# A two-layer decoder trunk on one core: tile starts at multiples of 512 bytes, half-tiles of the next stage ahead of the last transposes, other homes for the last groups' weights

## The chip, the core and the metric

The kernel runs on one core of one Trainium2 chip. The core has TensorE for matrix products (PE in the profile, with its weight loads as PEld), VectorE (DVE), ScalarE (ACT), GpSimd (POOL) and SyncE (SP, which here only issues DMAs). The metric is the device time of one execution in microseconds (us); lower is better. Before the change the median of three runs is 3107.32 us (3106.07 to 3114.94). Chances below speak of faster or slower by over 0.3%, which is about 9.3 us.

## The reference

The input is one sequence of 1024 positions with 1024 features, float32, and a memory of 256 tokens. Two layers follow each other; each is

```python
mix, xq = mixer(x)                                   # layer 0: gated delta rule; layer 1: S5 scan
cross = memory_attention(xq, mem, w_kv[i])           # 4 heads of 128
h = concatenate([mix, cross]) @ w_o[i]               # 1536 -> 1024
x = layer_norm(1.414 * x + h, ln1_g[i], ln1_b[i])
f = square(relu(x @ mlp_w1[i])) @ mlp_w2[i]          # 1024 -> 4096 -> 1024
x = layer_norm(1.414 * x + f, ln2_g[i], ln2_b[i])
```

The mixer of layer 0 is a gated DeltaNet (8 heads of 128, a short convolution on q, k and v, a chunked recurrence). That of layer 1 is a diagonal state-space layer (64 groups of 16 channels, a complex state of 64 each), followed by `z * sigmoid(z @ w_glu + b)`.

## The kernel before

**Arithmetic.** Large products run in the type float32r. Each operand is split into a high part `hi` (a copy rounded to float32r, by ACT) and a low part `lo` (the difference, by DVE). A product is three matmuls into the same PSUM bank (`mm3`, lines 110 to 116): hi times hi on L114, hi times lo on L115, lo times hi on L116. The moving operand is 512 columns wide, the stationary one 128 by 128. Small products (the recurrences, the S5 blocks, the transposes) are plain float32.

**Layouts.** Activations that go into a projection lie feature-major in `xT`: per half `h` of the 1024 positions a `hi` and a `lo` tile of 8 blocks of 512 columns, so four tiles. Results that are added up lie position-major in `y`, 8 blocks `tau` of 128 positions.

**Homes.** One SBUF pool holds a fixed number of buffers for each tag (`TAGS`): six `xT` of 16 KB a partition, two `raw`, four `w1`, seven `h1`, nine `h2`, seven `h3`, six `h4`, five `h5`, two `gb`, one `scr`, six `S`. A buffer is as large as the largest tile of its tag, and buffers lie one after another behind the constants. Sizes before: `s5t` (2T + 2·8·129 floats) makes an `xT` buffer 16448 bytes; the convolution's `cv` (3 + T floats) makes a `gb` buffer 4128 bytes after rounding; `H1` (4·9·16 floats) makes an `h5` buffer 2304 bytes; `scr` has 5280 bytes. As the tags follow each other, in the built program every tile of a large matmul starts at an odd multiple of 32 bytes: 224 past a multiple of 512 for `w1` and `h1`, 416 past one for `h2`, `h3` and `h4`, and 32 to 480 past one for the six `xT` buffers.

**Weights.** `load_split` (L86) reads 128 rows of a weight into a `raw` buffer (SP queue), makes one 1024-wide `hi` (ACT, L93) and `lo` (DVE, L94). `load_split2` (L98) does the same in two halves of 512 (ACT L106, DVE L107), each with a home of its own.

**Stages.** The order is: layer 0's mixer and attention (0 to about 830 us); `out_proj` of layer 0 with the first layer norm; the MLP of layer 0 (about 990 to 1771 us) with `s5_side`, which prepares tables and matrices of S5 beside the first 13 blocks; `mem_kv` and the S5 stage of layer 1 (to about 2110 us); `glu`; `out_proj` of layer 1; the MLP of layer 1 (about 2370 us to the end).

**Out projection and MLP.** `out_proj` (L798) takes the 12 row blocks of the concatenated outputs in four groups of two and a last group of four; the MLP (L186) takes the 32 blocks of 128 hidden features in 14 groups of two and a last group of four. In each group the weights are loaded, in the MLP the hidden block is projected (`proj_fm`, matmuls named `w`), and then for each `tau` two banks are summed by `acc_tm` (matmuls named `tm`) and added to `y` by DVE. In the last group each `tau` is finished by `done`: a layer norm on DVE and POOL (L160 to L170), a store where there is one, and `transpose_x` (L172), which is eight transposes on PE (`xt`, L180) and two `hi`/`lo` pairs (L182, L183) into the new `xT`. The next stage's first projection needs the new `xT`: its half 0 is there after `tau` 3, its half 1 after `tau` 7.

The order on each engine is fixed at build time by the tile framework, which follows the program's order as a priority and places an instruction where it expects its operands to be ready. At the end of layer 0's `out_proj` PE's order is: eight transposes of `tau` 6, two `w`, eight transposes, two `w`, and so on; the next group's first `w` follow behind the last transposes.

Lines that the change touches: `mlp`, `block_end`, `mlp_block`, `out_proj`, `combine`, `s5_mats`, `s5_u`, `s5_core`, `run`, and the sizes in `conv_silu` and `gdn_consts`.

Of the kernel before, what the change touches and what calls it, by code (L numbers as in the profile page):

```python
# [16 lines left out]
P = 128  # L17
# [11 lines left out]
class Trunk:  # L29
    def __init__(self, ctx, tc, a):  # L30
        self.tc = tc
        self.nc = nc = tc.nc
        self.a = a
        self.uid = 0
        self.turn = 0
        self.proj = 0
        self.cp = ctx.enter_context(tc.tile_pool(name="cp", bufs=1))
        self.sp = ctx.enter_context(tc.tile_pool(name="sp", bufs=1))
        self.ps = ctx.enter_context(tc.tile_pool(name="ps", bufs=1, space=bass.MemoryType.PSUM))
        self.dp = ctx.enter_context(tc.tile_pool(name="dp", bufs=1, space=bass.MemoryType.DRAM))  # L40
# [78 lines left out]
    def new_xT(self):  # L119
        return [tuple(self.tile("xT", [P, KT, HALF], F32R, f"xT{p}{h}") for p in "hl") for h in range(2)]  # L120

    def proj_fm(self, src, xT, evac, nm, banks=("mm",)):

        w = src if isinstance(src, tuple) else self.load_split(src, "w1", nm)
        for h in range(2):
            self.proj += 1
            ps = self.psum(banks[self.proj % len(banks)], nm)
            for k in range(KT):
                c = slice(k * P, (k + 1) * P)
                self.mm3(ps, (w[0][:, c], w[1][:, c]), (xT[h][0][:, k, :], xT[h][1][:, k, :]), k == 0, k == KT - 1)  # L130
            evac(h, ps)
# [54 lines left out]
    def mlp(self, i, xT, y, done, side=None):  # L186
        nc = self.nc
        blocks = [(2 * n, 2 * n + 1) for n in range(14)] + [(28, 29, 30, 31)]
        for fb, fs in enumerate(blocks):
            last = len(fs) == 4  # L190
            wk = [self.load_split2(self.a["w2"][i, f], ("h1", "h2", "h2", "h5")[j], "w2") for j, f in enumerate(fs)]
            hk = []
            for j, f in enumerate(fs):
                hs = [None, None]

                def evac(h, ps):
                    nc.scalar.activation(ps, ps, AF.Relu)  # L197
                    nc.scalar.activation(ps, ps, AF.Square)
                    hi = self.tile("h1" if j == 3 and h else "h3", [P, HALF], F32R, "hh")
                    lo = self.tile("h1" if j == 3 else "h4", [P, HALF], F32R, "hl")  # L200
                    nc.scalar.copy(hi, ps)  # L201
                    nc.vector.tensor_tensor(lo, ps, f32(hi), op=ALU.subtract)  # L202
                    hs[h] = (hi, lo)

                self.proj_fm(self.a["w1"][i, f], xT, evac, "w1", ("mm", "mm", "pa"))
                hk.append(hs)
            for tau in range(8):
                def add(c, ps):
                    o = y[tau][:, c * HALF:(c + 1) * HALF]
                    if fb == 0:  # L210
                        nc.vector.scalar_tensor_tensor(o, o, ALPHA, ps, op0=ALU.mult, op1=ALU.add)
                    else:
                        nc.vector.tensor_tensor(o, ps, o, op=ALU.add)  # L213
# [586 lines left out]
    def out_proj(self, i, y, done, early):  # L800
# [3 lines left out]
        for gi, ks in enumerate(order):  # L804
            last = len(ks) == 4
            wk, hk = [], []
            for j, k in enumerate(ks):
                tag = ("w1", "h5", "h2", "h2")[j] if early and last else "w1" if early and gi % 2 == 0 else \
                    ("h1", "h5")[j] if early else ("h1", "h2", "h2", "h5")[j]
                if tag == "w1":  # L810
                    hi, lo = self.load_split(self.a["w_o"][i, k], "w1", "wo")
                    wk.append([(hi[:, c * HALF:(c + 1) * HALF], lo[:, c * HALF:(c + 1) * HALF]) for c in range(2)])
                else:
                    wk.append(self.load_split2(self.a["w_o"][i, k], tag, "wo"))
            if early and not last:
                hq = self.tile("xT", [P, KT, HALF], F32R, "chl")
            for j, k in enumerate(ks):
                r = self.load_raw(self.cat[k * P:(k + 1) * P], "cat")
                hs = []
                if j == 3 and not early:  # L820
                    hq = [self.tile("w1", [P, 1024], F32R, "chl") for _ in range(2)]
                for h in range(2):
                    s = r[:, h * HALF:(h + 1) * HALF]
                    if early and not last:
                        hi, lo = hq[:, 4 * j + 2 * h, :], hq[:, 4 * j + 2 * h + 1, :]
                    elif j == 3 and not early:
                        hi, lo = (q[:, h * HALF:(h + 1) * HALF] for q in hq)
                    else:
                        hi = self.tile("h1" if j == 3 else "h3", [P, HALF], F32R, "ch")
                        lo = self.tile("h1" if j == 3 else "h4", [P, HALF], F32R, "cl")  # L830
# [171 lines left out]
    def combine(self, eng, x, y, pr, pi, op, b, nm):  # L1002

        n = pr.shape[1]
        o, w = (self.tile("h5", [P, 4, n, 16], F32, z) for z in (nm, "cw"))
# [33 lines left out]
    def s5_mats(self, m, b, co):  # L1039
# [7 lines left out]
        h1 = self.combine(V, co[:, 2], co[:, 3], re[:, :, gl], im[:, :, gl], A_, b, "H1")  # L1047
        nc.gpsimd.dma_start(self.h1d[m, :, gs], h1)
        dd = self.dd(8 * m + 4 * b)
        pz = self.psum("pa", "pz", (P, 4, 8, 16))  # L1050
        for g in range(4):
            nc.tensor.matmul(flat(pz[:16, g]), co[:, 0, 4 * b + g, :], flat(h1[:, g, 0:8, :]), start=True, stop=False)
# [14 lines left out]
    def s5_u(self, m, xT):  # L1067
        nc = self.nc
        u = self.s5t[:, 0:T]
# [4 lines left out]
        self.proj_fm(self.a["w_in5"][m], xT, evac, "wu")  # L1074
        nc.sync.dma_start(self.ud[m].rearrange("s c n -> c s n"), u.rearrange("p (s n) -> p s n", s=8))

    def s5_core(self, m):
# [4 lines left out]
        u = self.s5t[:, 2 * T + 8 * 129 * (m % 2):2 * T + 8 * 129 * (m % 2 + 1)].rearrange("p (g n) -> p g n", g=8)  # L1082
        V.memset(u[:, :, 0:1], 0.0)
        nc.sync.dma_start(u[:, :, 1:129], self.ud[m].rearrange("s (i g) n -> (s i) g n", i=16))
# [3 lines left out]
        for b in range(2):  # L1088
# [18 lines left out]
            for g in range(4):  # L1107
                nc.tensor.matmul(p1[:, g, :], G1[:, g], u[:, 4 * b + g, 0:128], start=True, stop=True)
            for g in range(4):
                nc.tensor.matmul(p2[:, g, :], G2[:, g], u[:, 4 * b + g, 0:128], start=True, stop=True)  # L1110
# [54 lines left out]
    def run(self):  # L1165
# [36 lines left out]
        xT = self.block_end(0, y)  # L1202
# [3 lines left out]
        xT = self.mlp_block(0, y, xT, self.s5_side, lambda tau: nc.sync.dma_start(self.x2[tau], y[tau]), True)  # L1206
        kv = self.mem_kv(1)
        self.s5t = self.tile("xT", [P, 2 * T + 2 * 8 * 129], F32, "s5t")
        self.s5_u(0, xT)
        for m in range(8):  # L1210
            if m < 7:
                self.s5_u(m + 1, xT)
# [7 lines left out]
        xT = self.block_end(1, y)  # L1220
        out = a["out"].rearrange("(n s) d -> s n d", s=8)
        self.mlp_block(1, y, xT, None, lambda tau: nc.sync.dma_start(out[tau], y[tau]), False)

    def block_end(self, i, y):

        xT = []

        def done(tau):
            if not xT:
                xT.extend(self.new_xT())  # L1230
# [5 lines left out]
        return xT  # L1236

    def mlp_block(self, i, y, xT, side, store, more):
        new = []

        def done(tau):
# [6 lines left out]
            if more:  # L1248
                self.transpose_x(y[tau], tau, new)

        self.mlp(i, xT, y, done, side)
# [89 lines left out]
```

## Time and profile before

| | |
|---|---|
| median of three runs | 3107.32 us |
| profiled execution | 3115.24 us |
| its span, first to last instruction | 3113.5 us |
| PE busy | 2892.1 us, 93% |
| DVE busy | 1762.9 us, 57% |
| ACT busy | 964.6 us, 31% |
| POOL busy | 488.4 us, 16% |
| mean granted TensorE clock | 0.967 of full |

Matmuls overlap in the array, so a matmul's listed duration (about 0.4 us for 512 columns) is longer than the distance from its start to the next one's. The distance, taken from starts in the timeline or from the number of matmuls in a stretch, is what adds up to time.

### The profile page before, as it was taken

The numbers are of one execution on the slowest core, as the hardware profiler recorded it, in microseconds if no ns is written. First come the engines' busy times: TensorE is split into PE (matmuls) and PEld (weight loads), VectorE is DVE, ScalarE is ACT, GpSimd is POOL, SyncE is SP. The second block draws the span as 40 slices with busy tenths as digits, with TensorE's granted clock in tenths as the row PEclk, the third lists the DMA queues.
The fourth block names the chain that finished last, engine by engine and source line by source line (L and its number), as shares of the span: only waits on it lengthen the run. The fifth ranks groups of instructions, "written<-read, shape, count | busy, mean of one in ns | idle before, by whom it ended". The sixth has DMA issues, their size and how long they took to land. (4 is left out here: it accounts for less than half of the span.)

```text
span 3113.5 us, 36492 instructions
## 1 busy us (share of the span) xinstructions
PE 2892.1 (93%) x13629; PEld 2311.9 (74%) x13629; DVE 1762.9 (57%) x3452; ACT 964.6 (31%) x2070; POOL 488.4 (16%) x729
## 2 busy tenths in 40 slices
PE   8789898898998999999999989987999999999998
PEld 6568676676777888777777767765777888888876
DVE  7635766765578677666663733443467344334436
ACT  5334444443422322232222222332222222222221
POOL 3620633625001021110100100011000000000001
PEclk9889999999999999999999999998999999999999
DMA  5322433333522133222221365554321111111111
GB/s 193 101 58 82 115 105 101 99 105 77 179 82 76 42 108 92 83 97 73 87 85 62 103 183 168 167 144 142 108 95 61 48 48 43 53 48 48 41 48 54
DMA packets 204145, 288.11 MB, mean 93 GB/s; under 512 B 85776, under 2 KB 126944, under 8 KB 203968
## 3 DMA queue, kind: packets, MB, share of 16 engines
q1 hardware_dynamic: 188864, 245.46, 25.7%
q0 software_dynamic: 12800, 36.13, 3.9%
q10 hardware_dynamic: 2304, 4.20, 0.4%
q8 instruction: 107, 1.75, 0.2%
q14 instruction: 70, 0.57, 0.1%
HBM read 213.93 MB, written 71.79 MB: 92 GB/s over the span
## 5 line engine op out<-in xcount | busy, mean ns | idle before, releaser
L213 DVE TENSOR_TENSOR y<-tm,y 128x512 f32<-128x512 f32 x448 | 308.5, 690 | 223.0 <-PE tm L116 217.4
L114 PE MATMUL w<-xTh,w1h 128*128 128x512 f32 x1024 | 409.7, 400 | 14.9 <-ACT w1h L93 14.9
L116 PE MATMUL w<-xTh,w1l 128*128 128x512 f32 x1024 | 407.4, 398 | 4.5 <-DVE w1l L94 4.4
L114 PE MATMUL tm<-w2h,hh 128*128 128x512 f32 x1024 | 406.7, 398 | 0.0
L115 PE MATMUL w<-xTl,w1h 128*128 128x512 f32 x1024 | 406.6, 397 | 0.0
L116 PE MATMUL tm<-w2h,hl 128*128 128x512 f32 x1024 | 403.6, 395 | 0.0
L115 PE MATMUL tm<-w2l,hh 128*128 128x512 f32 x1024 | 402.1, 393 | 0.0
L106 ACT CAST w2h<-w2r 128x512 fp32r<-128x512 f32 x128 | 76.3, 619 | 588.7 <-PE tm L116 506.0
L114 PEld LDWEIGHTS w<-xTh,w1h 128*128 128x128 f32 x1024 | 194.1, 190 | 60.0 <-ACT w1h L93 16.2
L116 PEld LDWEIGHTS w<-xTh,w1l 128*128 128x128 f32 x1024 | 194.5, 190 | 52.0 <-DVE w1l L94 6.3
L115 PEld LDWEIGHTS w<-xTl,w1h 128*128 128x128 f32 x1024 | 194.2, 190 | 45.1
L116 PEld LDWEIGHTS tm<-w2h,hl 128*128 128x128 f32 x1024 | 192.1, 188 | 47.4 <-DVE hl L202 0.3
L114 PEld LDWEIGHTS tm<-w2h,hh 128*128 128x128 f32 x1024 | 192.2, 188 | 45.8 <-ACT hh L201 1.3
L115 PEld LDWEIGHTS tm<-w2l,hh 128*128 128x128 f32 x1024 | 192.7, 188 | 44.7
L167 POOL TENSOR_SCALAR mv<-mv 128x1 f32<-128x1 f32 x32 | 25.0, 780 | 1246.8 <-DVE mv L166 1246.8
L202 DVE TENSOR_TENSOR hl<-w,hh 128x512 fp32r<-128x512 f32 x128 | 87.2, 687 | 188.6 <-ACT hh L201 188.6
L94 DVE TENSOR_TENSOR w1l<-w1r,w1h 128x1024 fp32r<-128x1024 f32 x64 | 78.3, 1224 | 184.7 <-ACT w1h L93 184.7
L114 PE MATMUL wi<-xTh,wih 128*128 128x512 f32 x384 | 159.3, 415 | 3.5 <-ACT zc L640 3.5
L115 PE MATMUL wi<-xTl,wih 128*128 128x512 f32 x384 | 158.7, 413 | 0.0
L116 PE MATMUL wi<-xTh,wil 128*128 128x512 f32 x384 | 156.4, 407 | 0.0
L197 ACT ACTIVATE w<-w 128x512 f32<-128x512 f32 x128 | 74.5, 582 | 188.0 <-PE w L116 188.0
L93 ACT CAST w1h<-w1r 128x1024 fp32r<-128x1024 f32 x64 | 67.2, 1050 | 198.8 <-PE w L115 157.4
(414 smaller groups left out, 5791.3 us busy)
## 6 DMA issues: line engine op xcount, KB each, us to landing
w2r<-in_w_dram SPq DMA_DIRECT2D x64, 512.0 KB, 3.5
w1r<-in_w_dram SPq DMA_DIRECT2D x64, 512.0 KB, 3.5
wir<-in_w_in_dram SPq DMA_DIRECT2D x24, 512.0 KB, 3.7
wor<-in_w_o_dram SPq DMA_DIRECT2D x24, 512.0 KB, 3.5
cat<-cat SPq DMA_DIRECT2D x24, 512.0 KB, 3.4
gb<-gcd SPq DMA_DIRECT2D x32, 256.0 KB, 4.5
ntf<-nm POOLq DMA_DIRECT2D x32, 256.0 KB, 3.0
nm<-ntf SPq DMA_DIRECT2D x32, 256.0 KB, 3.4
```

The costliest lines, as they stand in the source:

```text
L93: nc.scalar.copy(hi, r)
L94: nc.vector.tensor_tensor(lo, r, f32(hi), op=ALU.subtract)
L106: nc.scalar.copy(hi, s)
L114: nc.tensor.matmul(ps, a[0], b[0], start=start, stop=False)
L115: nc.tensor.matmul(ps, a[0], b[1], start=False, stop=False)
L116: nc.tensor.matmul(ps, a[1], b[0], start=False, stop=stop)
L167: nc.gpsimd.tensor_scalar(mv[:, 2:3], mv[:, 1:2], 1e-5, None, op0=ALU.add)
L197: nc.scalar.activation(ps, ps, AF.Relu)
L202: nc.vector.tensor_tensor(lo, ps, f32(hi), op=ALU.subtract)
L213: nc.vector.tensor_tensor(o, ps, o, op=ALU.add)
```

## The change

Four things are done.

1. **Starts.** A constant `pad` of 112 floats is added, and sizes are changed so that each buffer is a multiple of 512 bytes: `scr` 11·P floats, `cv` T + P floats, `h5` 2048 bytes, `xT` 16384 bytes. Every tile of the large matmuls then starts at a multiple of 512 bytes. For `h5`, `H1` loses its ninth power: `combine` makes powers 0 to 7 in one call and power 8 in another, with small tiles under tag `S`, and the ninth goes to `h1d` by a DMA of its own. For `xT`, `s5t` loses the zero column in front of each group's 128 inputs: `u` has 128 columns, its `memset` goes, and the two state products are added into columns 1 to 127 of `py` instead of running on a shifted input.
2. **Order at three stage ends.** `proj_fm` is split, so that half `h` can be projected alone (`proj_half`). At the last `tau` of both `out_proj` and of layer 0's MLP, `last_x` runs: half 0 of the next stage's first block (24 matmuls), then the transposes of `tau` 6, half 0 of the next stage's second block (24 matmuls), then the transposes of `tau` 7. The next stage is the MLP (`mlp_front`: two blocks of `w1`) or S5 (`u_front`: `s5_u` of blocks 0 and 1, ahead of `mem_kv`). Their halves 1 come later. The new `xT` is taken half by half.
3. **The MLP's last group.** Of the four `w2` tiles two are loaded ahead, and the other two are loaded at the fourth block, behind the loads of three `w1` tiles, where all four came ahead of them before.
4. **The out projections' last group.** The weights' tags are `h5`, `h2`, `w1`, `w1` in layer 1 (before `h1`, `h2`, `h2`, `h5`) and `w1`, `w1`, `h2`, `h2` in layer 0 (before `w1`, `h5`, `h2`, `h2`). The split inputs of half 0 lie in one `xT` buffer, those of half 1 in `h3` and `h4`.

The core of the diff:

```diff
+        self.const("pad", [P, 112])
...
+    def proj_half(self, w, xT, h, nm, banks=("mm",)):
+        self.proj += 1
+        ps = self.psum(banks[self.proj % len(banks)], nm)
+        for k in range(KT):
+            t, c = (w[k // 4], k % 4) if isinstance(w, list) else (w, k)
+            c = slice(c * P, (c + 1) * P)
+            self.mm3(ps, (t[0][:, c], t[1][:, c]), (xT[h][0][:, k, :], xT[h][1][:, k, :]), k == 0, k == KT - 1)
+        return ps
...
+    def last_x(self, y, xT, work):
+        for tau in (6, 7):
+            next(work)
+            self.transpose_x(y[tau], tau, xT)
+
+    def mlp_front(self, i, xT, front):
+        ws = [self.load_split2(self.a["w1"][i, 0], "h1", "w1"), self.load_split(self.a["w1"][i, 1], "w1", "w1")]
+        hk = [[None, None] for _ in ws]
+        for j, w in enumerate(ws):
+            self.hidden(hk[j], j)(0, self.proj_half(w, xT, 0, "w1", self.W1_BANKS))
+            if j:
+                front.extend((ws, hk))
+            yield
...
-            wk = [self.load_split2(self.a["w2"][i, f], ("h1", "h2", "h2", "h5")[j], "w2") for j, f in enumerate(fs)]
+            load_w2 = lambda j: self.load_split2(self.a["w2"][i, fs[j]], ("h1", "h2", "h2", "h5")[j], "w2")
+            wk = [load_w2(0), load_w2(1)]
+            if fb == 0:
+                ws, hk = front
+                for j, w in enumerate(ws):
+                    self.hidden(hk[j], j)(1, self.proj_half(w, xT, 1, "w1", self.W1_BANKS))
+            else:
+                hk = []
+                for j, f in enumerate(fs):
+                    if j == 3:
+                        wk += [load_w2(2), load_w2(3)]
+                    hk.append([None, None])
+                    self.proj_fm(self.a["w1"][i, f], xT, self.hidden(hk[j], j), "w1", self.W1_BANKS)
...
-        scr = self.tile("scr", [P, 3 * P + 8 + 13 * 64 + 96], F32, "scr")
+        scr = self.tile("scr", [P, 11 * P], F32, "scr")[:, :3 * P + 8 + 13 * 64 + 96]
...
-        cv = self.tile("gb", [P, 3 + T], F32, "cv")
+        cv = self.tile("gb", [P, T + P], F32, "cv")[:, :3 + T]
...
-                tag = ("w1", "h5", "h2", "h2")[j] if early and last else "w1" if early and gi % 2 == 0 else \
-                    ("h1", "h5")[j] if early else ("h1", "h2", "h2", "h5")[j]
+                if last:
+                    tag = (("w1", "w1", "h2", "h2") if early else ("h5", "h2", "w1", "w1"))[j]
+                else:
+                    tag = "w1" if early and gi % 2 == 0 else ("h1", "h5" if early else "h2")[j]
...
-            if early and not last:
+            if early or last:
                 hq = self.tile("xT", [P, KT, HALF], F32R, "chl")
...
+                    if last and h == 0:
+                        hi, lo = hq[:, 2 * j, :], hq[:, 2 * j + 1, :]
...
-        h1 = self.combine(V, co[:, 2], co[:, 3], re[:, :, gl], im[:, :, gl], A_, b, "H1")
-        nc.gpsimd.dma_start(self.h1d[m, :, gs], h1)
+        h1 = self.combine(V, co[:, 2], co[:, 3], re[:, 0:8, gl], im[:, 0:8, gl], A_, b, "H1")
+        nc.gpsimd.dma_start(self.h1d[m, :, gs, 0:8], h1)
+        h8 = self.combine(V, co[:, 2], co[:, 3], re[:, 8:9, gl], im[:, 8:9, gl], A_, b, "H8", "S")
+        nc.gpsimd.dma_start(self.h1d[m, :, gs, 8:9], h8)
...
-        V.memset(u[:, :, 0:1], 0.0)
-        nc.sync.dma_start(u[:, :, 1:129], self.ud[m].rearrange("s (i g) n -> (s i) g n", i=16))
+        nc.sync.dma_start(u, self.ud[m].rearrange("s (i g) n -> (s i) g n", i=16))
...
-                nc.tensor.matmul(py[:, g, :], M0[:, 4 * b + g, :], u[:, 4 * b + g, 1:129], start=True, stop=False)
-                nc.tensor.matmul(py[:, g, :], H1[:, g], r1[:, g, :], start=False, stop=False)
-                nc.tensor.matmul(py[:, g, :], H2[:, g], r2[:, g, :], start=False, stop=True)
+                nc.tensor.matmul(py[:, g, :], M0[:, 4 * b + g, :], u[:, 4 * b + g, :], start=True, stop=False)
+                nc.tensor.matmul(py[:, g, 1:], H1[:, g], r1[:, g, 0:P - 1], start=False, stop=False)
+                nc.tensor.matmul(py[:, g, 1:], H2[:, g], r2[:, g, 0:P - 1], start=False, stop=True)
...
+        def u_front(xT):
+            self.s5t = self.tile("xT", [P, 4 * T], F32, "s5t")
+            self.us = [self.s5_u(m, xT) for m in range(2)]
+            for u in self.us:
+                next(u)
+                yield
...
-            self.transpose_x(y[tau], tau, xT)
+            if tau == 7:
+                self.last_x(y, xT, self.mlp_front(i, xT, front))
+            elif tau < 6:
+                self.transpose_x(y[tau], tau, xT)
```

In the built program PE's order at the end of layer 0's `out_proj` becomes: 22 `tm`, 24 `w`, 8 transposes, 24 `w`, 8 transposes, one `tm`, two `w`, two `tm`, 46 `w`, 93 `tm`. At the end of layer 0's MLP it becomes 24 `wu`, 8 transposes, 24 `wu`, 8 transposes, 48 `wu`, and then the 96 `mk` of `mem_kv`, which followed the transposes directly before.

More of the change, by code (lines that the diff above doesn't have):

```diff
@@ L125, in proj_fm @@
         for h in range(2):
[L126 to L131, printed above, removed]
+            evac(h, self.proj_half(w, xT, h, nm, banks))
     def quad(self, dt, nm):
@@ L183, in transpose_x, with hidden, evac, mlp @@
             nc.vector.tensor_tensor(lo[:, 4 * q:4 * q + 4, t0:t0 + P], ps, f32(o), op=ALU.subtract)
-    def mlp(self, i, xT, y, done, side=None):
+    def hidden(self, hs, j):
+        nc = self.nc
+        def evac(h, ps):
+            nc.scalar.activation(ps, ps, AF.Relu)
+            nc.scalar.activation(ps, ps, AF.Square)
+            hi = self.tile("h1" if j == 3 and h else "h3", [P, HALF], F32R, "hh")
+            lo = self.tile("h1" if j == 3 else "h4", [P, HALF], F32R, "hl")
+            nc.scalar.copy(hi, ps)
+            nc.vector.tensor_tensor(lo, ps, f32(hi), op=ALU.subtract)
+            hs[h] = (hi, lo)
+        return evac
+    W1_BANKS = ("mm", "mm", "pa")
+    def last_x(self, y, xT, work):
[10 more added lines that the diff above has]
+            yield
+    def mlp(self, i, xT, y, done, side, front):
         nc = self.nc
@@ L819, in out_proj @@
                 hs = []
-                if j == 3 and not early:
-                    hq = [self.tile("w1", [P, 1024], F32R, "chl") for _ in range(2)]
                 for h in range(2):
                     s = r[:, h * HALF:(h + 1) * HALF]
-                    if early and not last:
+                    if last and h == 0:
+                        hi, lo = hq[:, 2 * j, :], hq[:, 2 * j + 1, :]
+                    elif early and not last:
                         hi, lo = hq[:, 4 * j + 2 * h, :], hq[:, 4 * j + 2 * h + 1, :]
-                    elif j == 3 and not early:
-                        hi, lo = (q[:, h * HALF:(h + 1) * HALF] for q in hq)
-                    else:
-                        hi = self.tile("h1" if j == 3 else "h3", [P, HALF], F32R, "ch")
-                        lo = self.tile("h1" if j == 3 else "h4", [P, HALF], F32R, "cl")
+                    else:
+                        hi = self.tile("h3", [P, HALF], F32R, "ch")
+                        lo = self.tile("h4", [P, HALF], F32R, "cl")
                     nc.scalar.copy(hi, s)
@@ L1201, in run @@
             nc.sync.dma_start(y[tau], a["x"].rearrange("(n s) d -> s n d", s=8)[tau])
[L1202 removed]
+        xT, front = self.block_end(0, y)
         self.x2 = d("x2", [8, P, T])
         self.cat = d("cat1", [1536, T])
[L1206 removed]
+        def u_front(xT):
[3 more added lines that the diff above has]
+                next(u)
+                yield
+        xT = self.mlp_block(0, y, xT, front, self.s5_side, lambda tau: nc.sync.dma_start(self.x2[tau], y[tau]), u_front)
+        for u in self.us:
+            next(u)
         kv = self.mem_kv(1)
[L1208 to L1209 removed]
         for m in range(8):
[L1211 to L1212 removed]
+            if 0 < m < 7:
+                for _ in self.s5_u(m + 1, xT):
+                    pass
             self.s5_core(m)
@@ L1247, in done @@
             store(tau)
-            if more:
+            if more and tau == 7:
+                self.last_x(y, new, more(new))
+            elif more and tau < 6:
                 self.transpose_x(y[tau], tau, new)
-        self.mlp(i, xT, y, done, side)
+        self.mlp(i, xT, y, done, side, front)
         return new
```

51 lines of the change are left out of this document (22 added, 29 removed).

## The prediction

> **What bounds the kernel now.** I read the page first (span, engines, clock, costliest groups), then a table by stretches with each engine's busy time, then PE's timeline at the places where that table shows too little work, and last single lines.
>
> ```profile
> span 3113.5 us, 36492 instructions
> ...
> PE 2892.1 (93%) x13629; PEld 2311.9 (74%) x13629; DVE 1762.9 (57%) x3452; ACT 964.6 (31%) x2070; POOL 488.4 (16%) x729
> ...
> PEclk9889999999999999999999999998999999999999
> ...
> L213 DVE TENSOR_TENSOR y<-tm,y 128x512 f32<-128x512 f32 x448 | 308.5, 690 | 223.0 <-PE tm L116 217.4
> L114 PE MATMUL w<-xTh,w1h 128*128 128x512 f32 x1024 | 409.7, 400 | 14.9 <-ACT w1h L93 14.9
> ...
> L114 PE MATMUL tm<-w2h,hh 128*128 128x512 f32 x1024 | 406.7, 398 | 0.0
> ```
>
> PE is busy 93% of the span, and DVE's commonest step, the sum into `y`, waits for PE. So PE is the bound, in two ways: how far apart its matmuls start while it is fed, and the places where it isn't. The stretches (columns: length, busy us and instructions of PE, PEld, DVE, ACT, POOL, then the granted clock, DMA share, GB/s):
>
> ```profile
> 986.00:1002.00 16.00, 8.74 (x39) 6.82 (x39) 14.42 (x20) 4.98 (x8) 4.68 (x8) 0.68 0.25 87
> 1667.00:1677.00 10.00, 4.20 (x11) 2.63 (x10) 4.94 (x7) 3.27 (x5) 0.00 (x0) 0.66 0.56 187
> 1769.00:1784.00 15.00, 8.37 (x45) 7.23 (x44) 11.84 (x19) 4.76 (x8) 2.71 (x3) 0.77 0.61 212
> 2308.00:2321.00 13.00, 7.71 (x23) 5.80 (x23) 6.66 (x11) 4.70 (x9) 0.00 (x0) 0.74 0.58 200
> 2365.00:2381.00 16.00, 9.33 (x35) 7.35 (x34) 13.50 (x18) 5.11 (x8) 2.38 (x3) 0.68 0.53 165
> 2500.00:2900.00 400.00, 400.00 (x1721) 323.27 (x1720) 165.37 (x233) 101.68 (x162) 0.00 (x0) 1.00 0.14 48
> 3003.00:3016.00 13.00, 7.14 (x19) 4.86 (x18) 5.44 (x7) 3.23 (x4) 0.00 (x0) 0.74 0.60 194
> ```
>
> The sixth row is an MLP in steady state: 1720 matmuls in 400 us, one every 232.5 ns, PE never idle, clock 1.00. The other six rows are the places the change touches: PE works about half of each, and the granted clock falls to 0.66 to 0.77 there. PE's timeline at them (start, duration, and in brackets the idle time before and who ended it):
>
> ```profile
> 986.07 1.03 PE L180 MATMUL xt<-ident,y 128*128 128x128 f32 x8
> 986.86 0.47 PE L114 MATMUL tm<-woh,ch 128*128 128x512 f32 x1
> ...
> 991.74 1.94 PE L180 MATMUL xt<-ident,y 128*128 128x128 f32 x8 [2.79 <-DVE y L170]
> 998.08 0.79 PE L116 MATMUL w<-xTh,w1l 128*128 128x512 f32 x1 [4.40 <-DVE w1l L94]
> ...
> 1673.54 0.80 PE L114 MATMUL w<-xTh,w1h 128*128 128x512 f32 x1 [5.76 <-ACT w1h L93]
> ...
> 1777.86 1.94 PE L180 MATMUL xt<-ident,y 128*128 128x128 f32 x8 [5.58 <-DVE y L170]
> ...
> 2313.73 0.80 PE L114 MATMUL tm<-woh,ch 128*128 128x512 f32 x1 [5.29 <-ACT ch L831]
> ...
> 2375.17 1.94 PE L180 MATMUL xt<-ident,y 128*128 128x128 f32 x8 [3.39 <-DVE y L170]
> ...
> 3009.49 0.80 PE L114 MATMUL w<-xTh,w1h 128*128 128x512 f32 x1 [5.83 <-ACT w1h L93]
> ```
>
> At the three stage ends (986, 1769, 2365) PE stands before transposes whose layer norm isn't done; at the three last groups (1667, 2308, 3003) it stands before weights or inputs whose split came late. To price a stretch I take from its length what its PE work would need at full speed: 0.2325 us per 512-column matmul, 0.10 per transpose (eight from 986.07 to 986.86), 0.114 per 256-column `mk` (rows below). Lost at 986: 16 less 15 matmuls and 24 transposes (3.5 + 2.4) = 10.1. At 1667: 10 less 11 matmuls = 7.4. At 1769: 15 less 8 matmuls, 16 transposes and 21 `mk` (1.9 + 1.6 + 2.4) = 9.1. At 2308: 13 less 23 = 7.7. At 2365: 16 less 19 and 16 transposes (4.4 + 1.6) = 10.0. At 3003: 13 less 19 = 8.6. Together 53 us, with the slow clock after each stall.
>
> **The change part by part: order and homes.** The split of `proj_fm` puts 24 matmuls (5.6 us) ahead of the transposes of `tau` 6 and 24 ahead of those of `tau` 7. At 986 the last `tm` ends near 988.3 and `y` of `tau` 6 is there at 991.7: the first 24 cover that. How long the next one takes is DVE's matter:
>
> ```profile
> L164 DVE BATCH_NORM_STATS2 bn<-y 128x6 f32<-128x512 f32 x64 | 42.3, 681 | 0.4
> L170 DVE SCALAR_TENSOR_TENSOR y<-y,mv,gb 128x1024 f32<-128x1024 f32 x32 | 40.9, 1278 | 2.9 <-POOL mv L168 2.9
> L183 DVE TENSOR_TENSOR xTl<-xt,xTh 128x512 fp32r<-128x512 f32 x48 | 30.8, 681 | 3.0 <-ACT xTh L182 2.6
> ```
>
> A `tau` costs DVE two sums (0.69 each), two statistics (0.68), two 1024-wide steps (1.28; L169 has L170's form) and two `lo` (0.68): 6.7 us. So `tau` 7 is ready at about 998.5, and PE, after 48 matmuls and 8 transposes from 988.3, at 1000.4: no wait. Next late is half 1, which needs the two `hi`/`lo` pairs of `tau` 7, about 2 us after the transposes. I leave 2 us at each of the three ends: 6 of 53 stay. At the last groups all loads are issued earlier or into homes that are free; I take the stalls there as gone. What hides the loads is the group before (two blocks, over 20 us of PE). If a home isn't free, 5 to 6 us come back per place.
>
> New cost on those paths: the front projections put four hidden-block `lo` (0.68 us, the form of L183) on DVE ahead of the last norms, where DVE is 14.42 of 16 us busy: 2.7 us. On SP's queue the front's `w1` loads now stand ahead of the next `w2`, and in the last group two `w2` stand behind three `w1`; they are needed only after all four projections, over 10 us later. With 1 us for the rest: 4 us. Net of this part: 53 − 6 − 4 = 43 us saved. Its ends: nothing saved at the last groups and a lost front (20) to all of 53.
>
> Elsewhere: `combine` for the ninth power is 16 calls more of three small DVE steps:
>
> ```profile
> L970 DVE TENSOR_TENSOR cs<-cs,ph x112: 156/184/420, 1090.3 to 1242.1; 128x4 f32<-128x4 f32 x16, 128x8 f32<-128x8 f32 x16, 128x16 f32<-128x16 f32 x16, 128x32 f32<-128x32 f32 x16
> ```
>
> 48 steps of some 0.2 us are 10 us of DVE beside the first MLP, where DVE waits for PE (L213 above); POOL's queue gets 16 small DMAs, in a stage where POOL has idle time. The shorter columns in `py`, eight fewer memsets: nothing measurable. If DVE lost its slack there, up to 10.
>
> **Starts at multiples of 512 bytes.** No engine's instruction count changes; the question is PE's distance. Four pairs of rows bound it:
>
> ```profile
> 1786.03 0.28 PE L114 MATMUL mk<-memh,wkh 128*128 128x256 f32 x1
> ...
> 1791.04 0.28 PE L116 MATMUL mk<-memh,wkl 128*128 128x256 f32 x1
> ...
> 2601.15 0.39 PE L116 MATMUL tm<-w2h,hl 128*128 128x512 f32 x1
> 2601.39 0.39 PE L114 MATMUL w<-xTh,w1h 128*128 128x512 f32 x1
> ...
> 3012.20 0.63 PE L116 MATMUL w<-xTh,w1l 128*128 128x512 f32 x1
> ...
> 3013.91 0.63 PE L114 MATMUL w<-xTh,w1h 128*128 128x512 f32 x1
> ```
>
> From 3012.20 to 3013.91, at half clock, four distances of 0.427: twice 213.5, so at full clock 19 of 232.5 ns are not columns but something that shows only there. From 1786.03 to 1791.04 there are 44 distances of 113.9 ns for 256 columns, 227.7 per 512, with other starts of both operands. Single distances in the MLP read 0.23 or 0.24. So the distance depends on operands by some nanoseconds, and starts are a candidate. The trace has no row with both operands of a 512-wide matmul at a multiple of 512 bytes. Its price lies between 213.5 and 240. I take 227.5, the nearest row of another placement: 5 ns less.
>
> How many such matmuls stand on the path (each row times three, for L114 to L116):
>
> ```profile
> L114 PE MATMUL wi<-xTh,wih 128*128 128x512 f32 x384 | 159.3, 415 | 3.5 <-ACT zc L640 3.5
> ...
> L114 PE MATMUL tm<-woh,ch 128*128 128x512 f32 x240 | 96.9, 405 | 7.2 <-ACT ch L831 7.2
> ...
> L114 PE MATMUL tm<-woh,chl 128*128 128x512 f32 x144 | 59.0, 411 | 3.3 <-ACT chl L831 3.3
> ...
> L114 PE MATMUL wg<-xTh,wgh 128*128 128x512 f32 x128 | 51.7, 404 | 14.2 <-ACT wgh L93 14.2
> ...
> L114 PE MATMUL wu<-xTh,wuh 128*128 128x512 f32 x128 | 51.0, 399 | 0.0
> ```
>
> `w` and `tm` of the MLPs 6144, `tm` of the out projections 1152, `wg` and `wu` 768: 8064, times 5 ns = 40 us. The 1536 of the first mixer (`wi` and `wz`, 128 a line) stand beside a recurrence and count half: 4 us.
>
> **Sum.** 43 + 44 = 87. Against the profiled span of 3113.5 (3115.24 with what lies around it) that is 3026 and 3028; the profiled run is 8 us above the median of 3107.32, against which the forecast stands: 3020.
>
> **Rivals.**
>
> *Pure columns.* The starts cause all of the 19 ns. 8064 × 19 = 153, and 1536 at half weight 15, less some 15 in the last groups, where DVE's 6.7 us a `tau` sets the pace (768 matmuls). With the 43: 196, so 2911. For it: the half-clock distance is pure columns, so nothing fixed stands in the way. Against it: a cost that a better start removes whole is seen nowhere in the trace. The Trainium skill ("TensorE: Matmul & The Clock Gate", section "Wait — 56ns, not 53.3ns?") gives 426.7 ns cold and 215.7 warm for 512 columns. This trace agrees cold (427) and disagrees warm (232.5); by the page's warm figure 8064 matmuls would save 135 us.
>
> *Starts do nothing.* Then only the stalls go: 3064, or 3086 if half of them stay. For it, one family of rows with many starts:
>
> ```profile
> L1110 PE MATMUL p<-s5t,G x128: 270/275/275, 1838.1 to 2080.9; 128*128 128x128 f32 x128
> ```
>
> Its moving `u` starts at 16 offsets, 516 bytes apart, and the durations are 270 to 275. Against it: these are plain float32 matmuls of 128 columns, and the stationary operand had one placement. The Trainium skill ("SBUF — State Buffer", section "Specifications (TRN2)") counts 16-byte lines and a penalty at each cross to a new line. All starts before are already multiples of 32 bytes, so by that rule a 512-byte start gains nothing. The trace can't decide it.
>
> *Slower: one phase collides.* With every start at the same place of 512 bytes, the moving read, the weight load (PEld is at 323 of 400 us) and the writes of DVE and ACT may hit the same part of memory, and each matmul takes the worst distance read, 0.24: 7.5 ns × 9600 = 72 more, less 43: +29, 3136. It decides from 4.5 ns a matmul on, where the 43 are eaten. Against it: the distances spread little over six `xT` starts.
>
> **How the numbers follow.** Partial gain (3020) has 0.32, its own range 2995 to 3060; pure columns (2911) 0.26; nothing from the starts (3064 to 3086) 0.28; collision 0.14, of which most ends slower. 2900 to 3090 leaves out the collision and little else. Within 0.3% (9 us) only where half the stalls stay and the distance grows a little: 0.04. Faster 0.82, slower 0.14.
>
> **What would show it.** In the sixth stretch's counterpart, 1758 matmuls in 400 us mean 227.5 ns; 1720 mean that starts do nothing; 1860 pure columns; under 1667 the collision. Each of the six stretches should lose under 3 us, PE's row before the transposes of `tau` 7 should show no wait for L170, and the rows after 1673 and 3009 none for L93 over 1 us. The forecast is wrong if the distance leaves 224 to 231 ns, or if loads for the front wait for homes.

## The result, and the profile after

The changed kernel takes 3017.99 us (median of four, 3012.86 to 3021.85) against 3108.95 for the kernel before on the same chip: a ratio of 0.9704, 95% interval 0.9683 to 0.9725, 91 us less. In a second comparison it was 3016.59 us and again 0.9704 (0.9686 to 0.9722). The profiled execution is the fastest of the first four, 3012.86 us.

The page after (span; busy times; granted clock; costliest groups). L115 to L117 are the three matmuls that were L114 to L116, L252 is the sum that was L213:

```profile
span 3010.8 us, 36564 instructions
...
PE 2832.7 (94%) x13629; PEld 2297.6 (76%) x13629; DVE 1765.6 (59%) x3491; ACT 964.1 (32%) x2069; POOL 517.2 (17%) x745
...
PEclk9889999999999999999999999997999999999999
...
L252 DVE TENSOR_TENSOR y<-tm,y 128x512 f32<-128x512 f32 x448 | 307.8, 689 | 197.5 <-PE tm L117 193.8
L115 PE MATMUL w<-xTh,w1h 128*128 128x512 f32 x1024 | 401.7, 393 | 0.1
...
L115 PE MATMUL tm<-w2h,hh 128*128 128x512 f32 x1024 | 399.1, 390 | 0.0
```

The 14.9 us for which `w` waited on ACT's splits are 0.1, and one matmul is listed at 390 to 393 ns where it was 398 to 400. The table by stretches, at the same six places and in the steady MLP (columns as in the prediction):

```profile
969.00:985.00 16.00, 15.93 (x80) 13.12 (x78) 11.88 (x16) 5.84 (x11) 5.60 (x8) 1.00 0.24 71
1634.00:1644.00 10.00, 10.00 (x46) 8.29 (x45) 5.40 (x8) 0.00 (x0) 0.00 (x0) 1.00 0.18 52
1734.00:1749.00 15.00, 14.71 (x74) 12.08 (x72) 9.96 (x15) 3.75 (x7) 2.88 (x3) 1.00 0.66 224
2238.00:2251.00 13.00, 13.00 (x59) 10.78 (x58) 12.11 (x19) 5.62 (x9) 0.00 (x0) 1.00 0.57 183
2300.00:2316.00 16.00, 15.93 (x79) 13.14 (x78) 11.88 (x16) 6.13 (x11) 3.42 (x4) 1.00 0.41 130
2500.00:2900.00 400.00, 400.00 (x1767) 331.31 (x1766) 171.57 (x241) 104.47 (x166) 0.00 (x0) 1.00 0.15 49
2923.00:2936.00 13.00, 13.00 (x59) 10.74 (x59) 2.97 (x4) 4.75 (x8) 0.00 (x0) 1.00 0.13 42
```

PE is busy to 98% or more at all six, and the clock stays at 1.00 where it fell to 0.66 to 0.77. In 400 us of steady MLP the row counts 1767 matmuls where it counted 1721: one every 226.4 ns against 232.4 (from start to start in the traces, 226.7 against 232.7). PE's timeline at two of the stage ends shows what is left of the waits (in brackets; the rows without one waited for nothing):

```profile
977.30 1.03 PE L189 MATMUL xt<-ident,y 128*128 128x128 f32 x8
983.63 1.03 PE L189 MATMUL xt<-ident,y 128*128 128x128 f32 x8
...
1747.25 1.03 PE L189 MATMUL xt<-ident,y 128*128 128x128 f32 x8
1748.57 0.73 PE L115 MATMUL wu<-xTh,wuh 128*128 128x512 f32 x2 [0.29 <-ACT xTh L191]
```

One stretch became worse. Beside the first MLP's S5 tables PE was busy 447.7 of 450 us; now it is 439.0 (the three rows are the kernel before, the changed one, and the variant `h8_late` of the experiments):

```profile
1200.00:1650.00 450.00, 447.70 (x2075) 347.66 (x2074) 294.54 (x565) 120.23 (x197) 63.95 (x123) 1.00 0.26 86
```

```profile
1200.00:1650.00 450.00, 439.00 (x2048) 344.76 (x2047) 289.44 (x569) 117.53 (x193) 76.56 (x128) 0.99 0.25 85
```

```profile
1200.00:1650.00 450.00, 447.14 (x2102) 354.00 (x2101) 295.02 (x581) 124.21 (x204) 76.31 (x128) 1.00 0.26 88
```

The groups of that stretch name it. Before, the small products `pz` (L1052) and the transposes `pg` (L1060) stood 2.3 us; in the changed kernel, as L1093 and L1101, 11.0 us, 9.6 of them behind DVE:

```profile
L1052 PE MATMUL pz<-H,co 128*16 128x128 f32 x128 | 25.0, 277 | 1.1 <-DVE H L1011 1.1
...
L1060 PE MATMUL pg<-ident,G1T 128*128 128x128 f32 x64 | 9.7, 273 | 1.2 <-ACT z L1055 1.2
```

```profile
L1093 PE MATMUL pz<-H,co 128*16 128x128 f32 x128 | 25.0, 277 | 7.9 <-DVE H L1050 7.4
...
L1101 PE MATMUL pg<-ident,G1T 128*128 128x128 f32 x64 | 10.5, 290 | 3.1 <-DVE G1T L1050 2.2 <-ACT z L1096 0.7
```

By stages (starts of the matmuls in the two profiled executions): from the second layer's `out_proj` to the end 894.7 us became 845.5; from the first layer's `out_proj` to the last `tm` of its MLP 951.9 became 929.3; from there to `glu` 355.2 became 339.3; `glu` 93.4 became 90.6; the first mixer 818.3 became 805.9, but 814.1 in the second profiled execution of the same kernel, so most of these 12 us are one execution's. Over all the profiled variants the first mixer lies between 802.8 and 820.9 us.

### The profile page after: what moved, and what is told of

It reads as the page before. It is cut to its first block, busy times and chain, and to the rows that moved or that the text cites. A ratio compares the mean times of both kernels' runs of the same rounds, so it can differ in the third digit from the quotient of the medians.

```text
span 3010.8 us, 36564 instructions
## 1 busy us (share of the span) xinstructions
PE 2832.7 (94%) x13629; PEld 2297.6 (76%) x13629; DVE 1765.6 (59%) x3491; ACT 964.1 (32%) x2069; POOL 517.2 (17%) x745
## 5 line engine op out<-in xcount | busy, mean ns | idle before, releaser
L252 DVE TENSOR_TENSOR y<-tm,y 128x512 f32<-128x512 f32 x448 | 307.8, 689 | 197.5 <-PE tm L117 193.8
L115 PE MATMUL w<-xTh,w1h 128*128 128x512 f32 x1024 | 401.7, 393 | 0.1
L116 PE MATMUL w<-xTl,w1h 128*128 128x512 f32 x1024 | 400.7, 391 | 0.0
L117 PE MATMUL w<-xTh,w1l 128*128 128x512 f32 x1024 | 400.1, 391 | 0.0
L115 PE MATMUL tm<-w2h,hh 128*128 128x512 f32 x1024 | 399.1, 390 | 0.0
L116 PE MATMUL tm<-w2l,hh 128*128 128x512 f32 x1024 | 398.1, 389 | 0.0
L117 PE MATMUL tm<-w2h,hl 128*128 128x512 f32 x1024 | 397.3, 389 | 0.0
L176 POOL TENSOR_SCALAR mv<-mv 128x1 f32<-128x1 f32 x32 | 40.5, 1266 | 1165.9 <-DVE mv L175 1165.9
L117 PEld LDWEIGHTS w<-xTh,w1l 128*128 128x128 f32 x1024 | 192.8, 188 | 40.9 <-issue 0.8
L115 PEld LDWEIGHTS w<-xTh,w1h 128*128 128x128 f32 x1024 | 192.8, 188 | 40.7 <-ACT xTh L191 0.8
L115 PEld LDWEIGHTS tm<-w2h,hh 128*128 128x128 f32 x1024 | 192.3, 188 | 41.3 <-ACT hh L204 1.4
L116 PEld LDWEIGHTS w<-xTl,w1h 128*128 128x128 f32 x1024 | 192.9, 188 | 39.9 <-issue 0.4
L117 PEld LDWEIGHTS tm<-w2h,hl 128*128 128x128 f32 x1024 | 192.1, 188 | 40.2 <-DVE hl L205 0.3
L116 PEld LDWEIGHTS tm<-w2l,hh 128*128 128x128 f32 x1024 | 192.3, 188 | 39.6
L115 PE MATMUL wi<-xTh,wih 128*128 128x512 f32 x384 | 158.6, 413 | 2.3 <-ACT zc L679 2.3
L116 PE MATMUL wi<-xTl,wih 128*128 128x512 f32 x384 | 158.1, 412 | 0.0
L117 PE MATMUL wi<-xTh,wil 128*128 128x512 f32 x384 | 156.4, 407 | 0.0
```

The lines of the kernel that those rows point to most:

```text
L115: nc.tensor.matmul(ps, a[0], b[0], start=start, stop=False)
L116: nc.tensor.matmul(ps, a[0], b[1], start=False, stop=False)
L117: nc.tensor.matmul(ps, a[1], b[0], start=False, stop=stop)
L176: nc.gpsimd.tensor_scalar(mv[:, 2:3], mv[:, 1:2], 1e-5, None, op0=ALU.add)
```

## The experiments

The main theory was the prediction's: the distance between matmuls falls because of the starts, the stalls go because of the order and the homes, and the two add up. The rivals on trial were that only the order counts, that the starts must be multiples of 512, and that any common phase does.

**A map of starts.** A kernel that only streams, with no other engine at work.

```diff
...
+        for s in steps:
+            for m in steps:
+                self.series(m, m, s, s)
...
+        for m in steps:
+            self.series(0, m, 0, 0)
...
```

> A kernel that only streams: the data are loaded, then 350 series of 24 float32r matmuls (8 blocks of hi-hi, hi-lo, lo-hi, as in the projections) run with the start of the moving operands and of the stationary ones set to every pair of multiples of 32 bytes within 512, then each in steps of 4 bytes, then with 256 columns. No other engine works beside it; the output is not the reference's. Theory 'place': the distance depends on each operand's own start, 227 ns where both are multiples of 512 and up to 240 elsewhere. Theory 'equal phase': 227 wherever the two starts are equal, whatever they are. Theory 'traffic': without DVE, ACT and DMAs beside it the distance is one value everywhere, near 216.

Two neighbouring series of 24 in PE's timeline, each by its first and its last matmul's start: both starts 0, then the moving ones 32 bytes further.

```profile
48.20 0.39 PE L50 MATMUL bank<-big 128*128 128x512 f32 x1
...
53.42 0.39 PE L52 MATMUL bank<-big 128*128 128x512 f32 x1
53.64 0.40 PE L50 MATMUL bank<-big 128*128 128x512 f32 x1
...
59.01 0.40 PE L52 MATMUL bank<-big 128*128 128x512 f32 x1
```

23 distances in 5.22 us, 227 ns, and 23 in 5.37, 233.5. All 256 pairs, sorted by the moving start less the stationary one, modulo 256 bytes (mean of 32 pairs, and the least and greatest of them, from the starts in the trace):

```
difference   mean    least  greatest (ns)
  0          227.5   226.6  227.7
 32          233.3   233.2  233.4
 64          228.9   228.7  228.9
 96          233.9   233.3  233.9
128          233.3   232.3  233.4
160          234.1   233.9  234.3
192          233.3   233.1  233.4
224          233.0   232.8  233.0
```

In these series the difference decides within 1.1 ns; where both lie does not matter. So "equal phase" stands and "place" falls; "traffic" falls too, since the spread is there with all other engines idle and nothing comes near 216.

The table holds for series whose moving operands, high and low, share one start and whose stationary ones share one. Two other rows show that a matmul's own difference is not enough. In the first pair only the low moving operands lie 64 bytes further, so two of three matmuls have equal starts; it is the first and the last of 24. The second row is the first of 96 `tm` in the kernel before, whose last starts at 2601.15 (shown in the prediction):

```profile
1664.55 0.39 PE L50 MATMUL bank<-big 128*128 128x512 f32 x1
...
1669.88 0.39 PE L52 MATMUL bank<-big 128*128 128x512 f32 x1
```

```profile
2579.04 0.39 PE L114 MATMUL tm<-w2h,hh 128*128 128x512 f32 x1
```

The first are 23 distances in 5.33 us, 231.7 ns, where the table's 227.5 and 228.9 would give under 229. The others are 95 in 22.11 us, 232.8 ns. By the places given for the kernel before (stationary at 416, moving at 224 in `h1` and at 416 in `h2`), half of them have the difference 64 and half 0, so the table would again give under 229. One common start for all operands is what gives the short distance; how matmuls with different starts act on their neighbours, these runs don't show.

In steps of 4 bytes the distance lay between 226.7 and 240.0. With 256 columns the order is another: 120.0 ns at equal starts, 113.5 with the moving start 192 bytes further.

**The old starts in the new order.**

```diff
-        self.const("pad", [P, 112])
...
-        scr = self.tile("scr", [P, 11 * P], F32, "scr")[:, :3 * P + 8 + 13 * 64 + 96]
+        scr = self.tile("scr", [P, 3 * P + 8 + 13 * 64 + 96], F32, "scr")
...
-            self.s5t = self.tile("xT", [P, 4 * T], F32, "s5t")
+            self.s5t = self.tile("xT", [P, 4 * T + 16], F32, "s5t")
```

(and `cv` and the `h5` buffers back at their old sizes.)

> The changed kernel with each buffer back at the place it had before (pad out, sizes as before), the order of every engine unchanged. If the starts alone made the distance fall from 232.5 to 227 ns: 232 again, and 8064 x 5 ns = 40 us more, with the mixer's 4 us about 44, near 3060 us. If the shorter distance came with the new order (fewer stalls, other neighbours in time): no change, 3018.

3065.82 us, 0.9841 (0.9824 to 0.9858) of the kernel before, where the changed kernel is 0.9704: the starts alone are worth 0.0137 of 3109, 43 us (some 8 either way). The steady MLP is back at 231.2 ns a matmul by the count, not at the 232 of the kernel before:

```profile
2500.00:2900.00 400.00, 400.00 (x1730) 324.35 (x1729) 166.47 (x234) 101.61 (x162) 0.00 (x0) 1.00 0.15 48
```

**One phase, off the multiple.**

```diff
-        self.const("pad", [P, 112])
+        self.const("pad", [P, 104])
```

> The changed kernel with a pad of 104 instead of 112 floats: every start is 480 past a multiple of 512, all still equal, order unchanged. Theory 'place': a start off the multiple costs what it did before, 230 ns and more, 24 to 60 us. Theory 'equal phase': 227 ns and no change, 3018 us within 9.

3028.48 us, 0.9715 (0.9701 to 0.9730) on a chip where the kernel before took 3118.04; the changed kernel's 0.9704 lies inside. On the same chip it is 37 us under the run with the old starts. The steady MLP is as fast as with multiples of 512:

```profile
2500.00:2900.00 400.00, 400.00 (x1767) 331.20 (x1766) 169.09 (x237) 105.26 (x168) 0.00 (x0) 1.00 0.16 49
```

**The stage ends as before.**

```diff
-            if tau == 7:
-                self.last_x(y, xT, self.mlp_front(i, xT, front))
-            elif tau < 6:
-                self.transpose_x(y[tau], tau, xT)
+            self.transpose_x(y[tau], tau, xT)
```

(and likewise in `mlp_block` and `mlp`; `u` of the first S5 block after `mem_kv`.)

> The changed kernel with the order of the three stage ends as before (no half projections ahead of the last transposes), starts and last groups as changed. The stalls at the ends should come back: 10.1 + 9.1 + 10.0 less the 2 left in the changed kernel, some 27 us, 3045 us. If the ends were bound by DVE's layer norms anyway: under 10.

3038.77 us, 0.9746 (0.9729 to 0.9762): 13 us over the changed kernel, half of what was expected (some 8 either way). PE's timeline shows why:

```profile
981.50 1.06 PE L189 MATMUL xt<-ident,y 128*128 128x128 f32 x8 [0.34 <-DVE y L179]
987.40 0.79 PE L117 MATMUL w<-xTh,w1l 128*128 128x512 f32 x1 [4.83 <-DVE w1l L95]
```

```profile
1762.84 1.94 PE L189 MATMUL xt<-ident,y 128*128 128x128 f32 x8 [5.58 <-DVE y L179]
...
2335.14 0.80 PE L117 MATMUL w<-xTh,w1l 128*128 128x512 f32 x1 [2.83 <-DVE w1l L95]
```

The wait for the norm of layer 0's `tau` 6 is 0.34 us where it was 2.79; only the end of the first MLP stands as long as before. The last groups' new homes had already shortened the other two: with both undone (`starts_only`, below) PE waits 2.81 and 4.84 us at the first of them, here 0.34 and 4.83, and 3.30 and 3.74 at the one near 2335, here 0.24 and 2.83.

**The last groups as before.**

```diff
-            wk = [load_w2(0), load_w2(1)]
+            wk = [load_w2(j) for j in range(len(fs))]
...
-                    if j == 3:
-                        wk += [load_w2(2), load_w2(3)]
```

(and the tags and split inputs of `out_proj`'s last group as in the kernel before.)

> The changed kernel with the homes, the split inputs and the load order of the last groups as before; starts and stage ends as changed. The three stalls of 7.4, 7.7 and 8.6 us at the last groups should come back: 24 us more than the changed kernel. Rival: the front's weights now need the same homes, so the stage ends suffer too, and it is 35 or more.

3035.46 us, 0.9773 (0.9753 to 0.9793): 0.0069, 21 us over the changed kernel, as expected; the rival of 35 falls. All three stalls are back where they were:

```profile
1648.41 0.79 PE L115 MATMUL w<-xTh,w1h 128*128 128x512 f32 x1 [5.82 <-ACT w1h L94]
...
2263.68 0.80 PE L115 MATMUL tm<-woh,ch 128*128 128x512 f32 x1 [5.46 <-ACT ch L868]
...
2933.33 0.80 PE L115 MATMUL w<-xTh,w1h 128*128 128x512 f32 x1 [6.02 <-ACT w1h L94]
```

**Both of these undone: the starts alone.** The edits of the last two together.

> The kernel before with the starts alone (pad, sizes, separate ninth power): stage ends and last groups as before. From the runs so far: 44 us less for the distance, some 14 more for the ninth power's steps: 30 us under the kernel before, ratio 0.990. If starts and order are not separate (the shorter distance needs the new order): no gain, 1.00 or above.

3074.04 us, 0.9876 (0.9862 to 0.9890), 38 us under the kernel before and 0.0172, 53 us, over the changed one. Order and homes together are worth some 53 us, though undone one by one they lose 13 and 21. That they overlap is seen one way: the homes shorten two of the stage ends. With the old last groups all three stalls stand in full, so the reverse isn't seen, and with some 8 us either way on each number the rest of the 19 stays open. The starts gain 38 here, 8 more than expected, and 43 in the new order. The two aren't the same sum: the 38 are net of the ninth power's extra steps (PE is busy 439.5 us between 1200 and 1650 us here too), while the 43 come from two kernels that both have them, with a distance that falls from 231.2 ns and not from 232.4.

**The ninth power later.** Two kernels: with its three DVE steps and its DMA behind the block's last ones, and with the DMA alone there.

```diff
-        h8 = self.combine(V, co[:, 2], co[:, 3], re[:, 8:9, gl], im[:, 8:9, gl], A_, b, "H8", "S")
-        nc.gpsimd.dma_start(self.h1d[m, :, gs, 8:9], h8)
...
         nc.gpsimd.dma_start(self.h2d[m, :, gs], h2.rearrange("p g e o -> p g (e o)"))
+        h8 = self.combine(V, co[:, 2], co[:, 3], re[:, 8:9, gl], im[:, 8:9, gl], A_, b, "H8", "S")
+        nc.gpsimd.dma_start(self.h1d[m, :, gs, 8:9], h8)
```

> The changed kernel with the ninth power and its DMA moved behind the rest of each block's S5 work, which reads nothing of it. The trace of the changed kernel shows about 16 us more stall on PE between 1200 and 1650 us than before, at the products that wait for DVE's H. If the ninth power on DVE and POOL's queue ahead of them is the cause: 8 to 16 us less than the changed kernel. If it is the faster matmuls alone that uncover DVE's pace: no change within 3 us.

3002.37 us, 0.9658 (0.9642 to 0.9674): 14 us under the changed kernel (some 8 either way), the fastest of all that were run. PE is busy 447.1 of the 450 us again (row above).

> The changed kernel with only the DMA of the ninth power moved behind the rest of each block's S5 work; its three DVE steps stay where they are. If POOL's queue (one more DMA ahead of the ones that free DVE's h5 homes) made the 14 us that moving both gave: the same 14 us less, ratio 0.966. If the three steps on DVE ahead of the products did, with the order on PE that the planner makes from them: no change against the changed kernel, 0.970.

3014.32 us, 0.9694 (0.9681 to 0.9707): no change. POOL's queue isn't the cause. What costs is the place of the three steps on DVE ahead of what PE waits for, together with the places that the tile framework gives the products on PE (it moved those too in `h8_late`, and not in this one); these two weren't separated.

**Multiples of 256, nine powers in one call.**

```diff
-        self.const("pad", [P, 112])
...
-        cv = self.tile("gb", [P, T + P], F32, "cv")[:, :3 + T]
+        cv = self.tile("gb", [P, T + 64], F32, "cv")[:, :3 + T]
...
-        h1 = self.combine(V, co[:, 2], co[:, 3], re[:, 0:8, gl], im[:, 0:8, gl], A_, b, "H1")
+        h1 = self.combine(V, co[:, 2], co[:, 3], re[:, :, gl], im[:, :, gl], A_, b, "H1")
```

> The changed kernel with each buffer a multiple of 256 bytes only, no pad (every start 64 past a multiple of 256) and the nine powers in one tile again, without the separate call and DMA. In the map the distance depends on the difference of the two starts modulo 256 alone, so it should stay 227 ns, and the 16 us of stalls beside S5's tables should shrink to some 5: 8 to 14 us under the changed kernel. If 512 matters: 230 ns and more, 24 us over it.

3015.62 us, 0.9700 (0.9685 to 0.9716): the distance is as forecast, the time isn't.

```profile
2500.00:2900.00 400.00, 400.00 (x1767) 331.20 (x1766) 170.85 (x240) 104.46 (x166) 0.00 (x0) 1.00 0.15 49
```

The matmuls `tm` of the first MLP take 738.9 us from first to last, as in `h8_late`, 11 less than in the changed kernel's second profile, and `pz` waits 1.6 us there where it waited 7.9: without the separate call that loss is gone too. But S5's stage is 4 us longer than there, the end of layer 0's `out_proj` 3 and the last norm 3. Why these three lose is open.

**What is left over 213.5.**

```diff
...
+        for cols in (128, 96, 64, 32):
+            for m in range(16):
+                self.series(big, 8 * m, 0, cols)
+        for m in range(16):
+            self.series(half, 16 * m, 0)
```

> Streams alone, as in the map of starts, no other engine beside them and an output that is not the reference's: 512 float32r columns against stationary operands of 128, 96, 64 and 32 columns, at moving starts 0 to 480 in steps of 32 bytes; then the same with bfloat16 operands of 128 columns, the moving start and then the stationary one stepped by 32 bytes. If the 13 ns left over 213.5 are the weight load meeting the moving read: the distance falls with the number of stationary columns, towards 214 at 32, and bfloat16 (a quarter of the traffic at half width each) comes near 216. If they are fixed to each matmul: 227 at every width.

The table by stretches with 32 and with 128 stationary columns, over all starts:

```profile
325.00:405.00 80.00, 80.00 (x347) 37.43 (x346) 0.00 (x0) 0.00 (x0) 0.00 (x0) 1.00 0.00 1
60.00:140.00 80.00, 80.00 (x346) 64.58 (x345) 0.00 (x0) 0.00 (x0) 0.00 (x0) 1.00 0.00 1
```

The weight loads fall from 64.6 to 37.4 us and the number of matmuls stays: 231 ns. So less to load doesn't bring the distance down to 214. That is the mean over sixteen starts; the gain from equal starts does depend on the width. This is the first and the last of the 24 with 32 stationary columns and equal starts:

```profile
321.31 0.39 PE L51 MATMUL bank<-big 128*32 128x512 f32 x1
...
326.63 0.39 PE L53 MATMUL bank<-big 128*32 128x512 f32 x1
```

23 distances in 5.32 us are 231 ns; with 96 and with 64 columns it is 230, and only with 128 is it 227. So the width of the stationary operand has a part in what the starts do; whether it is by way of its load, these runs don't say. The bfloat16 rows:

```profile
414.31 0.38 PE L52 MATMUL bank<-half 128*128 128x512 bf16 x1
...
416.47 0.38 PE L53 MATMUL bank<-half 128*128 128x512 bf16 x1
```

Ten distances in 2.16 us: 216 ns; of the 752 bfloat16 matmuls recorded, over all starts, nearly all follow at 215 to 216. So what is left belongs to float32r, or to operands of four bytes, and not to a matmul as such; by which mechanism, these runs don't say.

## Why the prediction was right, and where it was not

The forecast was 3020 and the time is 3018. Both halves went the forecast way. Two smaller terms were off and cancelled: the 10 us deducted from the stalls didn't show up in the runs, and the S5 tables, put at nothing, cost some 9 to 14. That the sum came within 2 us is luck.

*Stalls.* Forecast 53 − 6 − 4 = 43. Undoing order and homes together costs 53 (some 8 either way), so the sum of the stalls stands and the deductions don't. What was to remain, 2 us a stage end, is at most 0.3 (the `wu` row): the first of half 1 starts 1.3 us after the transposes, which fill 1.0 of that, since it needs only the first `hi`; the other parts arrive while it runs. The estimate let it wait for all of them. The 4 us of new cost were mostly four `lo` ahead of the last norms; in DVE's timeline the first of them starts at 980.23, behind the last norm's last step at 977.36 (2310.94 and 2308.07 in layer 1), and PE waits for neither. The two units can't be priced apart as I did, place by place: at 986 and 2365 part of the wait came from the last groups' late loads.

*Distance.* Forecast 227.5, 1758 matmuls in 400 us; measured 226.4 and 1767. Of the 44 us from it the experiment shows 43, against old starts that cost 231.2 ns in the new order. The value was near, the ground for it was weak: it came from 256-column matmuls, and the map shows these to go the other way with the start (120 where 512 columns are at their best). The row was near by luck. Two slips changed little: the sum leaves out the 384 matmuls of `wq` (2 us), and 400 us by 213.5 ns are 1873 matmuls, not 1860.

*The S5 tables.* This is the step that failed: "48 steps of some 0.2 us are 10 us of DVE beside the first MLP, where DVE waits for PE". DVE waits for PE there on average, but PE's products `pz` and `pg` need DVE's `H` and `G1T`, the new steps lie ahead of these, and PE stood 9 times, 9.6 us in all. PE lost 8.7 us busy in 450, and moving the steps gave 14 us (some 8 either way). The sum had put this at nothing; whether it exceeds the outer bound of 10 isn't settled.

*The mixer.* Forecast 4 us; the two profiles of the changed kernel show 12 and 4, and the other variants spread wider. Not settled.

*The rivals.* Pure columns: no pair of starts brings float32r under 226.6 ns. Its sum took the half-clock row for the floor at full clock. The warm figure in the Trainium skill ("TensorE: Matmul & The Clock Gate", section "Wait — 56ns, not 53.3ns?"), 215.7 ns, agrees with the bfloat16 rows (216) and not with float32r. Starts do nothing: 43 us speak against it, though the kernel before had them all at multiples of 32 bytes, and by the 16-byte lines of the Trainium skill ("SBUF — State Buffer", section "Specifications (TRN2)") nothing was to be gained from there. L1110, which spoke for it, has 128 columns of plain float32, and no run here tried that form. Collision: the common phase, which was to be the worst place, is the best of those tried.

## What to carry to other kernels

A distance between matmuls that is a few per cent over its columns is worth a map of its own: one common start for all operands gave some 40 us here. A constant shift of all buffers gives the same as a round address, and buffers that are multiples of 256 bytes do as well for the distance as multiples of 512. Map mixed starts too: a table from uniform ones doesn't price them. Price small steps on an engine with slack by who stands behind them, not by the mean share of busy time. Stalls that share a cause should be undone together before they are priced one by one.

## What the runs showed of the hardware

- Float32r matmuls of 512 columns and 128 stationary columns, in series whose moving operands share one start and whose stationary ones share one, follow 226.6 to 227.7 ns apart when the two starts are equal modulo 256 bytes, 228.7 to 228.9 with the moving one 64 bytes further, and 232.3 to 234.3 at the other multiples of 32.
- With mixed starts, equal ones of a single matmul aren't enough: 231.7 ns with only the low moving operand 64 bytes further, 232.8 for `tm` in the kernel before.
- With bfloat16 it is 215 to 216 at every start that was tried.
- With 256 columns equal starts are the slow ones: 120.0 ns against 113.5 at a difference of 192 bytes.
- Fewer stationary columns shorten the weight load (190 ns at 128, 108 at 32) and not the mean distance (231 ns); the gain from equal starts is there at 128 columns (227) and not at 32 (231).
